# Thirty-two experts on one core: up product ahead of its branch, transposes behind the other branch, down projection and gather between the two

## The chip, the cores and the metric

The kernel runs on one core of a Trainium2 chip, in one launch. The metric is the device time in microseconds, as the median of three runs of the kernel before: 2683.01 us (2674.14 to 2686.55).

## The reference, cut to what matters

Five transformer layers over 256 tokens of width 1024 come first; the change doesn't touch them. The last layer ends in a mixture of 32 experts, in which each token goes to 4:

```python
def clamped_swiglu(hgu):
    gate, up = jnp.split(hgu, 2, axis=-1)
    gate = jnp.minimum(gate, SWIGLU_LIMIT)
    up = jnp.clip(up, -SWIGLU_LIMIT, SWIGLU_LIMIT)
    return gate * jax.nn.sigmoid(SWIGLU_ALPHA * gate) * (up + 1)
...
    logits = (xt @ w_router + b_router).astype(jnp.float32)
    top_v, top_e = lax.top_k(logits, TOP_K)
    gates = jax.nn.softmax(top_v, axis=-1)
...
    def expert_block(args):
        xb, e = args
        return clamped_swiglu(xb @ w1[e] + b1[e]) @ w2[e] + b2[e]
```

Per expert w1 is 1024x2048 and w2 1024x1024, in float32, 12 MB together. How many tokens an expert has is known only at run time, from 0 to 256.

## The kernel before, in words

`experts` (from L1639) unrolls the 32 experts. An expert's tokens stand in slots of 32: the first 32 are always worked on (the main part), the others only inside branches `tc.If(n > 32)`, with inner ones for more than 64, 96 and 128 (`up_others` L1893, `down_others` L1875). Every engine evaluates the branch for itself from its own register. For expert e:

- `gather` (L1683) picks the rows of the tokens of two experts with one-hot matrices `Pq`, as products into a bank `g`; `modulate` (L1505) brings them into `xq`. `prep` (L1837) does half a pair in each step: part 0 in even experts, part 1 in odd ones, the latter followed by `prepare_sum` (L1848: `slot_gates`, `transposed`).
- `bias` (L1574) opens the accumulation in a bank `hg`, `up_proj` (L1728) adds x @ w1: 32 calls, 64 instructions of TensorE, on column quarters.
- `act_more`/`swiglu` (L1736): five instructions, VectorE and ScalarE in turn, from the bank into `um`. The main part fills rows 0 to 63 of `um`, the branch rows 64 to 127.
- `act_T` (L1744) transposes `um`, main and branch rows together, on TensorE, and copies the result into `aT`.
- `down` (L1857): `down_proj` of expert e-1 from `aT` into a bank `py` (64 instructions), its multiply by gate (L1868) and the split into two parts `ye`. `down_others(e-1)` does the other tokens, inside its branch, and adds them to `y` (`sum_more`).
- `scatter` (L1766): for a finished pair of experts, 32 products with the transposed one-hots into four banks, added to `y` by `take_in` (L1764).

The loop (L1932) traces them in this order: up branch of e, main up product, swiglu, down of e-1, down branch of e-1, bias of e+1, transposes, `prep`, on even e `scatter`. The engines' order is not the traced one: a scheduler picks, at build time, the instruction of highest priority (first traced) that is ready by its model; a branch is scheduled as one unit, with all that it reads. In the order that results, 56 of the 64 up instructions run ahead of the up branch and 8 behind it (those of the last weight chunk), and the transposes stand after a quarter of the down projection. `tc.issue_after(x)` puts instructions behind x on x's engine.

`announce` (L1723) issues a branch hint on TensorE's sequencer, behind a given instruction: that the jump over the branch is likely. Labels are `up{e}`, `down{e}` and the inner `down{e}.1`.

Weights come in chunks of 1 MB through a ring of 18 buffers, in SP's queue (`wload` L1399; w1 of e+1 ahead of w2 of e). A buffer is free when all its readers are done, the branch among them. PSUM banks: `hg` x2, `py` x2, `g` x2, and `hg0`, `hg1`, which belong to the branches (`banks` L1872).

Of the kernel before, what the change touches and what calls it, by code (L numbers as in the profile page):

```python
# [9 lines left out]
F32 = mybir.dt.float32  # L10
# [41 lines left out]
def tile_model(ctx: ExitStack, tc: tile.TileContext, A, out):  # L52
# [27 lines left out]
    ident = cb[:, 0:128]  # L80
# [54 lines left out]
    def mm(o, l, r, start=True, stop=True):  # L135
        return T.matmul(o, l, r, start=start, stop=stop)  # L136
# [1320 lines left out]
    def quarter(c):  # L1457
        return slice(32 * c, 32 * c + 32)
# [103 lines left out]
        V.tensor_scalar(rt["gate"][:, t], gr, left, None, ALU.mult)  # L1562

    def new_P():
        return rt["pool"].tile([128, 2, 128], F32, name="P2", tag="P2", bufs=2)

    def slices(j):
        return slice(64 * j, 64 * j + 64)
# [11 lines left out]
    def gtile():  # L1580
        return rt["pe"].tile([128, 512], F32, name="g", tag="g", bufs=2)

    def ytile():
        return rt["pe"].tile([128, 512], F32, name="py", tag="py", bufs=2)
# [54 lines left out]
    def experts(pos, gate, num):  # L1639
        h = xc  # L1640
        with ExitStack() as st:
# [110 lines left out]
            def down_proj(p, aT, e, c0=0, cs=range(4)):  # L1752

                first = None
                for kk in range(8):
                    for c in cs:
                        i = mm(p[quarter(c)], aT[:, kk % 4, c0 + 32 * (kk // 4):c0 + 32 * (kk // 4) + 32], w2_tile(e, kk, c), kk == 0, kk == 7)
                        first = first or i
                return first, i

            def take_in(c, p):

                cols = y[:, :, 256 * c:256 * c + 256]
                return V.tensor_tensor(cols, cols, p.rearrange("p (a b) -> p a b", b=256), op=ALU.add)  # L1764

            def scatter(gTs, yes):  # L1766

                ps = [ytile() for _ in range(2)] + [gtile() for _ in range(2)]
                for t in range(2):
                    for j in range(2):  # L1770
                        for i, part in enumerate(yes):
                            for c in range(4):
                                mm(ps[c][:, 256 * t:256 * t + 256], gTs[quarter(c), j, 128 * t:128 * t + 128], part[quarter(c), j], i + j == 0, i + j == 2)
                for c in range(4):
                    take_in(c, ps[c])


            def new_P1():
# [75 lines left out]

            yes = {}

            def down(e, aT):  # L1857

                j = e % 2
                if j == 0:  # L1860
                    yes[e // 2] = [ep.tile([128, 2, 256], F32R, name=f"ye{nm}", tag=f"ye{nm}") for nm in "hl"]
                gs = gTs[e // 2][1]
                while len(w2s.get(e, ())) < 4:
                    wload()
                p = ytile()[:, 0:256]
                _, last = down_proj(p, aT, e)
                w = ep.tile([128, 512], F32, name="gm", tag="gm")[:, 0:256]
                V.scalar_tensor_tensor(w, p, gs[:, 2 * j:2 * j + 1], g2, ALU.mult, ALU.mult)  # L1868
                two_parts(*[u[:, j] for u in yes[e // 2]], w)
                return last  # L1870

            def banks():  # L1872
                return [pe.tile([128, 512], F32, name=f"hg{g}", tag=f"hg{g}") for g in range(2)]
# [1 line left out]
            def down_others(e, aT, hg=None):  # L1875

                n, ums, ps = conds[e], umss[e % 2], banks()
                with tc.If(n > 32, label=f"down{e}"):
                    p = ps[1][:, 0:256]
                    announce(down_proj(p, aT, e, 64)[0], f"down{e}.1")  # L1880
                    bks = ps if hg is None else [ps[0], hg, ps[1]]
                    j = e % 2
                    sum_more(Pq[e // 2], 64 * j + 32, p, gTs[e // 2][1][:, 2 * j + 1:2 * j + 2], bks)
                    with tc.If(n > 64, label=f"down{e}.1"):
                        announce(down_more(e, 1, 0, ums[:, 0], ps), f"down{e}.2")
                        with tc.If(n > 96, label=f"down{e}.2"):  # L1886
                            announce(down_more(e, 1, 1, ums[:, 0], ps), f"down{e}.3")
                            with tc.If(n > 128, label=f"down{e}.3"):
                                for j in (2, 3):
                                    for g in range(2):  # L1890
                                        down_more(e, j, g, ums[:, j - 1], ps)

            def up_others(e):  # L1893

                n, ums, ps = conds[e], umss[e % 2], banks()
                with tc.If(n > 32, label=f"up{e}"):  # L1896
                    announce(bias(e, ps[0]), f"up{e}.1")
                    up_proj(w1s[e], ps[0], xq[e // 2][:, :, 64 * (e % 2) + 32:64 * (e % 2) + 64])
                    act_more(ps, 0, um, 1)
                    with tc.If(n > 64, label=f"up{e}.1"):  # L1900
                        announce(gather_more(e, 1, ps[1]), f"up{e}.2")
                        up_more(e, ps, 0)
                        act_more(ps, 0, ums[:, 0])
                        with tc.If(n > 96, label=f"up{e}.2"):
                            announce(up_more(e, ps, 1), f"up{e}.3")
                            act_more(ps, 1, ums[:, 0])
                            with tc.If(n > 128, label=f"up{e}.3"):
                                for j in (2, 3):
                                    gather_more(e, j, ps[1])
                                    for g in range(2):  # L1910
                                        up_more(e, ps, g)
                                        act_more(ps, g, ums[:, j - 1])
# [19 lines left out]
            for e in range(32):  # L1932
                hg = nxt
                while len(w1s.get(e, ())) < 8:
                    wload()
                if e == 0:
                    count(0)
                up_others(e)
                i = up_proj(w1s[e], hg, xq[e // 2][:, :, 64 * (e % 2):64 * (e % 2) + 32])
                if e:  # L1940
                    announce(i, f"down{e - 1}")
                if e == 0:
                    prepare_sum(0)
                act_more([hg], 0, um)
                nxt = htile() if e < 31 else None
                if e:
                    down(e - 1, aT)
                    down_others(e - 1, aT, nxt)
                if e < 31:
                    count(e + 1)  # L1950
                    announce(bias(e + 1, nxt), f"up{e + 1}")
                aT = act_T(um)
                if e < 30:
                    prep(e // 2 + 1, e % 2)
                if e:
                    if e % 2 == 0:
                        scatter(gTs.pop(e // 2 - 1)[0], yes.pop(e // 2 - 1))
                    if e == 20:
                        add_b2(umss[1])
                    if e == 30:  # L1960
                        ends = prepare_end(umss[1])
# [259 lines left out]
```

## Time and profile before

| what | value |
|---|---|
| median of 3 runs | 2683.01 us |
| the profiled execution | 2680.88 us |
| its span, first to last instruction | 2679.1 us |
| TensorE products, busy in the span | 2268.7 us (85%) |
| VectorE, ScalarE | 1208.1 us (45%), 714.7 us (27%) |
| the experts, 1285 to 2679.1 us | 1394 us |
| TensorE busy in these | 1052.74 us |
| mean granted clock in these | 0.82 (0.898 in the whole span) |
| mean DMA share and rate in these | 0.70, 281 GB/s |

PE is TensorE's products, PEld its weight loads, DVE VectorE, ACT ScalarE; a trailing q is an engine's sequencer. An idle time in a row is that of the engine ahead of the row's instructions, and behind the arrow stands what ended it: an engine with tile and line, a DMA, a sequencer, or "issue", where the profile shows nothing that was waited for. A product in float32 is two instructions in the trace. The granted clock is 1 at 2.4 GHz and 0.5 at 1.2 GHz.

### The profile page before, as it was taken

The page shows a single profiled execution, that of the slowest core. Times are in us where ns is not written, and L with a number is a line of the kernel's source. Part 1 is how long each engine was busy: PE and PEld are TensorE (multiplying, and loading weights), DVE is VectorE, ACT ScalarE, POOL GpSimd, SP SyncE. Part 2 cuts the span into 40 slices and gives each one's busy share as a digit, 9 for nine tenths or more (in the row PEclk, how much of TensorE's full clock was granted, in tenths as well). Part 3 has the DMA queues.
Part 4 walks back from the last instruction along what each step waited for, and adds up shares of the span by engine and source line. Part 5 has one row for each costly group of instructions (what it writes and reads, how often), then busy time and mean ns, then how long its engine had stood idle before and what let it go on. Part 6 is the DMA issues. An engine that isn't in the chain of part 4 may idle for free. (4 is left out here: it accounts for less than half of the span.)

```text
span 2679.1 us, 43271 instructions
## 1 busy us (share of the span) xinstructions
PE 2268.7 (85%) x17714; PEld 1491.4 (56%) x17714; DVE 1208.1 (45%) x2598; ACT 714.7 (27%) x1578; POOL 80.8 (3%) x125
## 2 busy tenths in 40 slices
PE   7999999989999998899887777877787776777776
PEld 4667777777897876785443343433343443433333
DVE  4877566576656886755322222222223232322222
ACT  4555544443345665424100000000000000000001
POOL 0000200000001000120000000000000000000000
PEclk9999999999999998999978888799887787787878
DMA  7434233333323554714774674599946274599966
GB/s 276 156 122 164 94 114 101 111 133 120 119 64 127 169 195 160 253 70 183 298 302 190 244 304 189 211 380 375 372 197 274 106 295 173 227 406 414 413 281 237
DMA packets 124861, 577.21 MB, mean 215 GB/s; under 512 B 11953, under 2 KB 12721, under 8 KB 91762
## 3 DMA queue, kind: packets, MB, share of 16 engines
q1 hardware_dynamic: 124530, 572.71, 56.3%
q8 instruction: 219, 3.59, 0.5%
q14 instruction: 112, 0.92, 0.1%
HBM read 571.61 MB, written 1.05 MB: 214 GB/s over the span
## 5 line engine op out<-in xcount | busy, mean ns | idle before, releaser
L136 PE MATMUL hg<-w,xq 128*32 128x512 f32 x2944 | 406.6, 664 | 40.6 <-PEq L1896 14.8
L136 PE MATMUL mm<-hT,wp 128*128 128x256 f32 (+1 forms) x1776 | 347.2, 340 | 0.6 <-DVE aqk L144 0.5
L136 PEld LDWEIGHTS mm<-hT,wp 128*128 128x128 f32 x1776 | 269.9, 189 | 52.8 <-issue 19.5
L136 PEld LDWEIGHTS hg<-w,xq 128*32 128x32 f32 x2944 | 112.5, 120 | 281.6 <-issue 236.5
L1738 DVE TENSOR_SCALAR gm<-hg 64x512 f32<-64x512 f32 x51 | 34.8, 683 | 416.3 <-PE hg L136 410.7
L111 DVE TENSOR_TENSOR wp<-w,wp 128x1024 fp32r<-128x1024 f32 (+2 forms) x149 | 177.7, 1198 | 71.7 <-ACT wp L110 70.5
L136 PE MATMUL mm<-wp,hT 128*128 128x256 f32 (+1 forms) x1584 | 194.0, 281 | 6.7 <-DVE mixT L419 3.0
L136 PEld LDWEIGHTS mm<-wp,hT 128*128 128x128 f32 x1584 | 187.0, 189 | 12.5 <-DVE wp L111 3.4
L110 ACT ACTIVATE wp<-w 128x1024 fp32r<-128x1024 f32 (+2 forms) x149 | 153.8, 1036 | 97.8 <-PE mm L136 50.1
L1739 ACT ACTIVATE um<-gm 64x512 f32<-64x512 f32 x46 | 28.9, 629 | 543.2 <-DVE gm L1738 543.2
L136 PE MATMUL py<-w,aT 128*32 128x256 f32 x2048 | 163.0, 445 | 6.5 <-issue 3.5
L136 PEld LDWEIGHTS py<-w,aT 128*32 128x32 f32 x2048 | 73.3, 128 | 85.4 <-issue 54.9
L136 PE MATMUL g<-P,xc 128*128 128x128 f32 x496 | 102.5, 381 | 20.7 <-issue 12.9
L1748 PE MATMUL g<-cb,um 128*128 128x128 f32 x128 | 30.4, 382 | 101.6 <-DVE um L1742 101.6
L136 PEld LDWEIGHTS g<-P,xc 128*128 128x128 f32 x496 | 94.0, 287 | 31.3 <-issue 26.7
L1512 DVE TENSOR_SCALAR xq<-g,modA,modB 128x128 f32<-128x128 f32 x62 | 25.4, 409 | 168.7 <-PE g L136 153.3
L1510 ACT ACTIVATE xq<-g,modB,modA 128x128 f32<-128x128 f32 x62 | 28.3, 457 | 271.3 <-DVE xq L1512 271.3
L136 PE MATMUL hg<-w,aT 128*32 128x256 f32 x896 | 64.5, 429 | 32.1 <-issue 32.1
L136 PE MATMUL ada<-w,scT 128*32 128x512 f32 x576 | 83.4, 623 | 6.6 <-DMA w<-l_w_ada 6.5
L1748 PEld LDWEIGHTS g<-cb,um 128*128 128x128 f32 x128 | 19.6, 190 | 113.3 <-issue 61.9
L136 PE MATMUL hg<-w,xs 128*32 128x512 f32 (+1 forms) x640 | 72.8, 615 | 3.1 <-ACTq L1886 1.1
L136 PE MATMUL hg<-ye,xs 32*128 32x256 f32 x304 | 53.0, 442 | 26.2 <-DVE xl L1764 14.3
(605 smaller groups left out, 3500.4 us busy)
## 6 DMA issues: line engine op xcount, KB each, us to landing
w<-w SPq DMA_DIRECT2D x383, 1024.0 KB, 14.1
w<-l_w_ada SPq DMA_DIRECT2D x96, 512.0 KB, 4.4
w<-w_ada SPq DMA_DIRECT2D x48, 512.0 KB, 4.2
w<-l_w_z SPq DMA_DIRECT2D x32, 512.0 KB, 4.3
w<-l_w_out SPq DMA_DIRECT2D x32, 512.0 KB, 4.1
w<-l_w_q SPq DMA_DIRECT2D x16, 512.0 KB, 5.0
w<-l_w_v SPq DMA_DIRECT2D x12, 512.0 KB, 5.5
w<-w_dqkv SPq DMA_DIRECT2D x12, 512.0 KB, 4.5
```

The costliest lines, as they stand in the source:

```text
L110: S.activation(hi, src, AF.Copy)
L111: V.tensor_tensor(lo, src, hi, op=ALU.subtract)
L136: return T.matmul(o, l, r, start=start, stop=stop)
L1510: S.activation(dst[:, i, :], src[:, i, :], AF.Identity, scale=a[:, k], bias=b[:, k])
L1512: V.tensor_scalar(dst[:, i, :], src[:, i, :], a[:, k], b[:, k], ALU.mult, ALU.add)
L1738: V.tensor_scalar(gm, gate, 7.0, None, ALU.min)
L1739: S.activation(um, gm, AF.Sigmoid, scale=1.702)
L1748: T.transpose(tp[:, q * 128:(q + 1) * 128], um[:, q * 128:(q + 1) * 128], ident)
```

## The change

The main up product and its swiglu are traced ahead of the up branch. The bank `p` of the down projection is claimed ahead of that branch, and the branch writes a column of it, so that the down projection stays behind the branch. Between the two branches stand, in this order: on odd e from 3 to 29 the scatter of the pair before last (it was on even e), now in the branches' two banks and two of `g`; the down projection of e-1; behind its last product the gather of `prep`. After the down branch come bias of e+1, the up hint, and behind the bias the transposes of e. The down hint of e-1 goes behind the first product of scatter or down; the inner hint `down{e}.1` behind the last product of the branch's down projection instead of the first. `P2` has three buffers instead of two. Expert 30 still scatters at its end.

```diff
-        return rt["pool"].tile([128, 2, 128], F32, name="P2", tag="P2", bufs=2)
+        return rt["pool"].tile([128, 2, 128], F32, name="P2", tag="P2", bufs=3)
...
             def scatter(gTs, yes):
-                ps = [ytile() for _ in range(2)] + [gtile() for _ in range(2)]
+                ps, first = banks() + [gtile() for _ in range(2)], None
...
-                                mm(ps[c][:, 256 * t:256 * t + 256], gTs[quarter(c), j, 128 * t:128 * t + 128], part[quarter(c), j], i + j == 0, i + j == 2)
+                                k = mm(ps[c][:, 256 * t:256 * t + 256], gTs[quarter(c), j, 128 * t:128 * t + 128], part[quarter(c), j], i + j == 0, i + j == 2)
+                                first = first or k
...
+                return first
...
-            def down(e, aT):
+            def down(e, aT, p):
...
-                p = ytile()[:, 0:256]
-                _, last = down_proj(p, aT, e)
+                first, last = down_proj(p, aT, e)
...
-                return last
+                return first, last
...
-                    announce(down_proj(p, aT, e, 64)[0], f"down{e}.1")
+                    announce(down_proj(p, aT, e, 64)[1], f"down{e}.1")
...
-            def up_others(e):
+            def up_others(e, p=None):
...
                 with tc.If(n > 32, label=f"up{e}"):
+                    if p is not None:
+                        mm(p[:, 0:1], ident, ident[:, 0:1])
...
-                up_others(e)
-                i = up_proj(w1s[e], hg, xq[e // 2][:, :, 64 * (e % 2):64 * (e % 2) + 32])
+                up_proj(w1s[e], hg, xq[e // 2][:, :, 64 * (e % 2):64 * (e % 2) + 32])
+                act_more([hg], 0, um)
+                p = ytile()[:, 0:256] if e else None
+                up_others(e, p)
+                nxt = htile() if e < 31 else None
+                first = last = None
+                if e % 2 and e > 1:
+                    first = scatter(gTs.pop(e // 2 - 1)[0], yes.pop(e // 2 - 1)) if e < 31 else None
                 if e:
-                    announce(i, f"down{e - 1}")
-                if e == 0:
+                    i, last = down(e - 1, aT, p)
+                    announce(first or i, f"down{e - 1}")
+                    with tc.issue_after(last.ins):
+                        if e < 30:
+                            prep(e // 2 + 1, e % 2)
+                    down_others(e - 1, aT, nxt)
+                else:
                     prepare_sum(0)
-                act_more([hg], 0, um)
-                nxt = htile() if e < 31 else None
-                if e:
-                    down(e - 1, aT)
-                    down_others(e - 1, aT, nxt)
+                    prep(1, 0)
                 if e < 31:
                     count(e + 1)
-                    announce(bias(e + 1, nxt), f"up{e + 1}")
-                aT = act_T(um)
-                if e < 30:
-                    prep(e // 2 + 1, e % 2)
+                    i = bias(e + 1, nxt)
+                    announce(i, f"up{e + 1}")
+                    with tc.issue_after(i.ins):
+                        aT = act_T(um)
+                else:
+                    aT = act_T(um)
                 if e:
-                    if e % 2 == 0:
+                    if e == 30:
                         scatter(gTs.pop(e // 2 - 1)[0], yes.pop(e // 2 - 1))
```

## Rows read from the trace of the kernel before

**Rows 1.** The page: span, and the granted clock in 40 slices, in tenths.

```profile
span 2679.1 us, 43271 instructions
...
PEclk9999999999999998999978888799887787787878
```

**Rows 2.** Waits of TensorE, 1285 us to the end: total us, times, longest.

```profile
PE g L1748 <- DVE um L1742: 101.6, 31, 5.2
...
PE hg L136 <- PEq L1878: 33.2, 14, 4.6
...
PE hg L136 <- PEq L1896: 14.8, 14, 4.2
...
PE hg L136 <- DVE um L1741: 11.6, 4, 2.9
```

**Rows 3.** Timeline of TensorE around a taken branch: start us, us, idle before.

```profile
1403.90 7.04 PE L136 MATMUL hg<-w,xq 128*32 128x512 f32 x62
...
1412.37 1.05 PE L136 MATMUL py<-w,aT 128*32 128x256 f32 x16
1418.58 1.09 PE L1748 MATMUL g<-cb,um 128*128 128x128 f32 x4 [5.15 <-DVE um L1742]
1419.46 2.77 PE L136 MATMUL g<-P,xc 128*128 128x128 f32 x12
1422.16 1.94 PE L136 MATMUL py<-w,aT 128*32 128x256 f32 x16
...
1424.79 1.07 PE L136 MATMUL py<-w,aT 128*32 128x256 f32 x16
```

**Rows 4.** Timeline of TensorE behind a skipped branch.

```profile
1533.91 1.08 PE L1748 MATMUL g<-cb,um 128*128 128x128 f32 x4 [2.85 <-DVE um L1742]
```

**Rows 5.** Timeline of VectorE at the wait of Rows 3.

```profile
1413.10 0.69 DVE L1741 TENSOR_SCALAR um<-hg 64x512 f32<-64x512 f32 x1
...
1414.93 0.68 DVE L1738 TENSOR_SCALAR gm<-hg 64x512 f32<-64x512 f32 x1 [0.41 <-DVEq L1900]
...
1417.75 0.68 DVE L1742 SCALAR_TENSOR_TENSOR um<-um,gm 64x512 f32<-64x512 f32 x1
```

**Rows 6.** Groups of TensorE, 1285 us to the end: busy, mean ns | idle before.

```profile
L136 PE MATMUL hg<-w,aT 128*32 128x256 f32 x896 | 64.5, 429 | 32.1 <-issue 32.1
...
L136 PE MATMUL py<-yeh,gTq 32*128 32x256 f32 x120 | 32.2, 379 | 9.2 <-DVE gm L1868 9.2
...
L136 PE MATMUL hg<-cb,P 128*32 128x128 f32 x304 | 17.6, 289 | 5.5 <-issue 5.5
```

**Rows 7.** Stretches: length, busy PE, PEld, DVE, ACT, POOL, clock, DMA share, GB/s.

```profile
1418.60:1424.20 5.60, 5.60 (x33) 4.11 (x34) 0.00 (x0) 0.00 (x0) 0.00 (x0) 0.50 1.03 416
1533.90:1537.00 3.10, 3.09 (x15) 3.10 (x16) 0.00 (x0) 0.00 (x0) 0.00 (x0) 0.51 0.91 330
1784.00:1945.00 161.00, 120.77 (x1233) 62.73 (x1236) 41.11 (x80) 12.36 (x25) 0.00 (x0) 0.87 0.94 377
2360.00:2560.00 200.00, 145.55 (x1387) 72.24 (x1382) 45.35 (x92) 16.08 (x32) 0.00 (x0) 0.81 1.02 413
2200.00:2350.00 150.00, 112.73 (x1116) 59.73 (x1119) 40.84 (x82) 9.63 (x19) 0.00 (x0) 0.79 0.56 221
```

**Rows 8.** Waits of TensorE, 2360 to 2560 us.

```profile
PE g L1748 <- DVE um L1742: 13.5, 6, 2.9
```

**Rows 9.** Waits of TensorE, 1784 to 1945 us.

```profile
PE g L1748 <- DVE um L1742: 9.6, 3, 4.4
```

**Rows 10.** Branch evaluations on TensorE's sequencer: ns min/median/max, first and last start.

```profile
L1896 PEldq COMPARE_BRANCH  x32: 74/412/6217, 1297.6 to 2639.9; - x32
...
L1878 PEldq COMPARE_BRANCH  x32: 74/400/5626, 1329.7 to 2667.9; - x32
...
L1884 PEldq COMPARE_BRANCH  x24: 69/198/369, 1340.5 to 2623.0; - x24
```

## The prediction

> **What bounds the kernel now.** I read the page first. The span is 2679.1 us, and from the slice at 20 of 40 on (the experts, 1285 us to the end; their first up branch is evaluated at 1297.6 [rows 10]) the granted clock of TensorE is 7 to 8 tenths where it was 9 before [rows 1]. The profiled execution took 2680.88 us, 1.8 us more than its span and 2.1 us less than the median of the runs, 2683.01. Next the waits of TensorE in the experts' stretch: the largest by far is that of the activation transposes of `act_T` for the last swiglu instruction (L1742 on VectorE), 101.6 us in 31 waits [rows 2]. The timeline of TensorE shows how one arises: the up product ends, 16 quarter-instructions of the down projection run in about 1 us, and then the queue stands still until `um` is there: 5.15 us where the second branch ran (an expert with more than 32 tokens), 2.85 us where it was skipped [rows 3, 4]. The reader is to see that the rest of the down projection and the gather, which need no `um`, stand behind the waiting transposes. The timeline of VectorE says why the wait is longer after a branch: the branch's own swiglu comes first, so that the main one starts at 1414.93 and ends at 1418.43, 7 us after TensorE had finished the branch's products [rows 3, 5].
>
> **The up product in front and the transposes at the end.** Nothing is computed less: the edit moves. After it, the main swiglu (about 3.5 us from its first instruction to its last, by the gap between 1414.93 and the end of the 1417.75 row [rows 5]) runs beside the branch or, where that is skipped, beside the down projection and the gather. The down projection is 64 instructions, and 16 take 1.07 us at the full clock, so 4.3 us; the gather of 16 instructions takes at least 3 us (12 of them 2.77 us) [rows 3]. Together 7 us in front of the transposes against 3.5 us of swiglu, and after a taken branch 7 us against the branch's own swiglu of about 3.5 us, the main one having run beside the branch's 62 products of 7.04 us. So I take the whole wait off: **-101.6**. If the scheduler, which orders by readiness, put the branch's swiglu still ahead of the main one, 7 us would stand against 7 us, so this term hardly depends on it.
>
> **The scatter.** It now stands on odd experts ahead of the down projection and writes the two banks `hg0`, `hg1`, which the branch's swiglu still reads. What is late next there: its first product must wait until the clip of `up` (L1741) has read the bank. The trace has that wait in one place, the second products inside the branch: 11.6 us in 4, 2.9 each [rows 2]. Fourteen experts take the branch (896 down products of 64 each in the branches [rows 6]), seven of them are odd and have a scatter (3, 7, 13, 15, 17, 19 and 29 by the timeline's branches): 7 x 2.9 = **+20**. Behind it wait down, gather and the branch on TensorE. In exchange the old scatter's wait for its `py` bank (9.2 us in all [rows 6]) goes: **-9**. VectorE's four additions of 512 columns after the scatter stand ahead of the multiply that empties the down projection's bank; at 0.7 us each, like the swiglu's steps of 512 columns [rows 5], they fit into that projection's 4.3 us: nothing.
>
> **The clock.** After each wait the granted clock is at its half level: 0.50 over the 5.6 us after the long wait, 0.51 over 3.1 us after the short one, with TensorE busy throughout [rows 7]; the same 16 products take 1.94 us there and 1.07 us a little later [rows 3]. So a long wait costs 2.8 us more, a short one 1.5. Thirteen long (over 4 us) and 17 short would be 62 us. I take 25: the seven scatter waits keep 1.5 each, the stretches below that are bound by DMA keep theirs, and instruction stalls nearby can hold the clock down. Bounds 0 and 62: **-25**.
>
> **The weights.** From 2360 to 2560 us the DMA share is 1.02 at 413 GB/s and from 1784 to 1945 it is 0.94 at 377 [rows 7]; a weight ring cannot give more there, so what TensorE saves it waits for the next chunk. These stretches hold 13.5 and 9.6 us of the 101.6 [rows 8, 9]. Earlier stretches leave the ring full, which could cover some; I give all back: **+23** (bounds 0 and 23, plus their part of the clock, counted above). The rest of the ring's order is as before: w1 chunks are still freed at the end of the up branch, w2 chunks at the end of the down branch, so SP's queue is not passed by anything.
>
> **The inner announcement.** Between the branch's down products TensorE stands for 32.1 us, released by nothing that the profile shows, and for 5.5 us more among the transposing products just behind [rows 6]. I take it for waiting for code: instructions come by DMA, in packets of 16 KB (219 of them are 3.59 MB [rows 1]). Today the hint for the inner jump is issued with the first product, and my reading is that the fetch it asks for goes ahead of the code about to run. Issued behind the last product it lets this code through first, which could give all 37.6 us. But the inner jump follows only some 4 us later, and a jump whose target isn't there has cost up to 6.2 us [rows 10]. It is skipped 10 times (24 evaluations, 14 first and 10 second [rows 10]). Half the stalls gone, 10 jumps late by 1.5 us: -19 + 15, **-4**; bounds -38 and +46 (10 x 4.6, the longest wait behind a down jump [rows 2]).
>
> **The other announcements.** The up hint now has the transposes and 64 products (136 instructions with the weight loads) ahead of its branch; the experts' waits behind these jumps are 14.8 us now [rows 2]. Before, the scatter stood in between on half of the experts. I add **+10**; bounds -15 and +55 (18 skipped branches x 4.2 us less the present wait). The down hint on odd experts is as far ahead of its branch as now, with the scatter added, so I leave the 33.2 us behind that branch [rows 2] as they are. What the hints are worth can be read: all evaluations of the inner branch, ten jumps among them, took 0.37 us at most, while the up and the down branch, hinted as well, took up to 6.2 and 5.6 us [rows 10]. So a hint helps in some places and is lost in others.
>
> The Trainium skill (Runtime: NRT & Kernel Launch, section Instruction fetch mechanics) says that instructions are prefetched in sequence only, two pages at a time, and that a jump out of these pages waits for a fetch. By that rule alone the hints would be worth nothing before and after, both announcement terms would be zero, the sum -92.6 and the time 2590 us; the trace's ten cheap inner jumps [rows 10] disagree, so the terms stay and rival (c) below has its chance from them.
>
> **Small ones together.** A third `P2` buffer, one 1-column product in each taken branch (14 in all, each shorter than the 0.29 us of a 128-column one [rows 6]), the claimed `py` bank (freed long before): nothing; even in full the products are 4 us.
>
> **Sum:** -101.6 + 20 - 9 - 25 + 23 - 4 + 10 = -86.6 us, so 2680.9 - 87 = 2594 on the profiled execution, and 2 us more on the median: **2596 us**.
>
> **Rivals.** (a) More comes back: half of the scatter waits is filled, the clock gives 45 instead of 25, the inner stalls go without late jumps (-30 instead of -4), the full ring covers half of the weights' part: 87 + 10 + 20 + 26 + 12 = 155, 2528 us. For it: the clock's level follows the waits in every row read. Against it: it takes four kind outcomes at once. (b) The weights take more: with experts coming faster, stretches that are now at half of the DMA, as 2200 to 2350 us at 0.56 [rows 7], become full as well where light experts lie in them. Of the 101.6 us then only the heavy experts' 13 long waits count, about 62 us, less 20 and with 10 of clock: 52, 2631 us. (c) The other side, **late jumps**: the place is the sequencer of TensorE at L1884, L1896 and L1878. If hints so close to their branch do nothing, each of 10 inner, 18 up and 9 even down skips (37) can cost 4.6 us and 1.5 us of half clock. The other terms give 101.6 - 20 + 9 + 25 - 23 = 93 us, so it decides from 15 late places on; at 20 places the time is 2683 + 122 - 93 = 2712 us. For it: up branches already take up to 6.2 us although they are hinted [rows 10]. Against it: the up hint of even experts and the down hint of even experts keep about as many instructions ahead of their branch as now. (d) The order isn't what the source says: the scheduler moves down and transposes so that TensorE waits for `um` again. The branch's product into `p` and the after-orders speak against it; then about 2683 us, no change.
>
> **Chances.** Forecast 0.58, (a) 0.14, (b) 0.14, (c) 0.08, (d) 0.06. Half a per cent (13 us) is what a measurement of this kernel can tell from no change. The first three are faster: 0.86; (d) is the same, 0.06; (c) slower, 0.08. The range leaves out (c), (d) and the outer part of (a): 2525 to 2660, from the sum with the kind ends of clock and inner hint to (b) with the up hint's dear half.
>
> **What would show it.** In the new profile the row L1748 <- L1742 should fall from 101.6 to a few us; the scatter's first products should show waits for L1741 of 2.9 in seven places; the granted clock of the work that now fills 2200 to 2350 us (0.79 now [rows 7]) should rise; "DMA w<-w" should grow as a releaser of up products; the 32.1 us between the branch's down products should halve, with waits named PEq L1884 in their place. The prediction is wrong if the L1748 wait stays above 40 us, or if PEq waits grow by more than 60 us, or if the wait moves to the `aT` copy or to the gather's one-hots.

## The result, and the profile after

The kernel after takes 2540.92 us (2537.56 to 2550.62), the kernel before, run beside it, 2678.57 us (2671.01 to 2686.55): a ratio of 0.949, with a 95% interval of 0.945 to 0.953. That is 5.1% faster. It lies inside the predicted range, 55 us below the predicted 2596 us, and nearer to rival (a). The profiled execution took 2538.24 us, 142.6 less than the one of before.

In the profile after some lines have moved: the up branch is L1897 (its swiglu parts L1903, L1907, L1910), the down branch L1879 (inner L1885, L1887, L1889), and the down projection's multiply L1869. The page, to set beside [rows 1]:

```profile
span 2536.5 us, 43274 instructions
...
PEclk9999999998999999999898788888888888788787
```

The clock of the experts' stage, from slice 20 on, has risen by less than a tenth. The stage is best weighed by stretches. The whole experts' stage of the kernel before (length, busy PE, PEld, DVE, ACT, POOL, clock, DMA share, GB/s):

```profile
1287.00:2679.00 1392.00, 1050.74 (x10209) 537.17 (x10208) 352.60 (x681) 108.87 (x214) 1.99 (x4) 0.82 0.70 281
```

and with only the instructions counted that touch the scatter's `gTq` (no POOL among them):

```profile
1287.00:2679.10 1392.10, 88.02 (x512) 65.65 (x512) 6.21 (x9) 4.56 (x8) 0.82 0.70 281
```

The same two views of the kernel after, the stage:

```profile
1297.00:2536.50 1239.50, 994.48 (x10235) 494.68 (x10234) 350.09 (x679) 106.50 (x213) 1.99 (x4) 0.84 0.79 315
```

and the scatter's part:

```profile
1297.00:2537.00 1240.00, 64.74 (x512) 54.08 (x512) 6.22 (x9) 4.56 (x8) 0.84 0.79 315
```

TensorE stood for 1392.0 - 1050.7 = 341.3 us before and for 1239.5 - 994.5 = 245.0 after: 96 us less. It was busy for 56 us less with the same products (but for the 1-column ones in the branches), 23 of them in the scatter. The stage began 10 us later in this execution, which the change doesn't touch. -96 - 56 + 10 is, but for rounding, the 142.6.

Waits of TensorE in the stage, after, to set beside [rows 2]:

```profile
PE g L136 <- issue: 38.4, 13, 5.2
PE hg L136 <- issue: 22.2, 10, 6.1
PE g L136 <- PEq L1879: 19.3, 9, 3.9
PE py L136 <- DMA w<-w: 19.1, 15, 2.8
PE hg L136 <- DVEq L1903: 16.2, 6, 2.7
PE hg L136 <- DVEq L1897: 14.0, 6, 3.2
...
PE hg L136 <- DMA w<-w: 12.9, 13, 1.5
PE hg L136 <- DVE um L1741: 11.7, 4, 2.9
PE py L136 <- PEq L1897: 10.8, 14, 2.7
PE g L136 <- PEq L1885: 9.1, 9, 5.4
```

The largest row of before, 101.6 us of transposes waiting for the swiglu, is gone from the list. Groups of TensorE in the stage, after (busy, mean ns | idle before), to set beside [rows 6]:

```profile
L136 PE MATMUL hg<-w,xq 128*32 128x512 f32 x2944 | 383.4, 630 | 13.0 <-DMA w<-w 12.9
...
L136 PE MATMUL hg<-w,aT 128*32 128x256 f32 x896 | 57.5, 404 | 13.5 <-issue 13.5
...
L136 PE MATMUL hg<-yeh,gTq 32*128 32x256 f32 x124 | 27.4, 387 | 34.1 <-DVEq L1903 16.2 <-DVEq L1897 14.0 <-DVEq L1910 2.7
...
L1748 PE MATMUL g<-cb,um 128*128 128x128 f32 x128 | 26.4, 339 | 5.5 <-DVEq L1903 3.8 <-issue 1.8
L136 PE MATMUL g<-gate,P 128*32 128x1 f32 x1024 | 16.5, 186 | 28.7 <-issue 28.7
```

The transposes (L1748) still stand for 5.5 us. The scatter's first products (`hg<-yeh,gTq`) have a new wait of 34.1. The gate products of the gather waited before for ScalarE and hardly for anything unseen:

```profile
L136 PE MATMUL g<-gate,P 128*32 128x1 f32 x1024 | 11.7, 174 | 13.5 <-ACT xq L1510 13.0 <-issue 0.4
```

They now stand 28.7 us for nothing that the profile shows.

How the cover works is seen on VectorE, at the expert of [rows 3] and [rows 5], after:

```profile
1394.04 0.68 DVE L1738 TENSOR_SCALAR gm<-hg 64x512 f32<-64x512 f32 x1 [5.00 <-PE hg L136]
...
1396.87 0.68 DVE L1742 SCALAR_TENSOR_TENSOR um<-um,gm 64x512 f32<-64x512 f32 x1
1401.56 0.68 DVE L1738 TENSOR_SCALAR gm<-hg 64x512 f32<-64x512 f32 x1 [4.01 <-PE hg L136]
```

and on TensorE at the same time, with the place where the branch ends:

```profile
1394.44 7.04 PE L136 MATMUL hg<-w,xq 128*32 128x512 f32 x64
...
1405.28 0.75 PE L136 MATMUL hg<-yeh,gTq 32*128 32x256 f32 x2 [2.69 <-DVEq L1903]
```

The main swiglu ends at 1397.55, while the branch's products run until 1401.5. What TensorE waits for behind the branch is now the branch's own swiglu, which frees the bank for the scatter: 2.69 us in place of 5.15.

### The profile page after: what moved, and what is told of

It is laid out like the page before. It is cut to its first block, busy times and chain, and to the rows that moved or that the text cites. A ratio compares the mean times of both kernels' runs of the same rounds, so it can differ in the third digit from the quotient of the medians.

```text
span 2536.5 us, 43274 instructions
## 1 busy us (share of the span) xinstructions
PE 2225.5 (88%) x17740; PEld 1456.0 (57%) x17740; DVE 1206.3 (48%) x2598; ACT 712.8 (28%) x1577; POOL 80.1 (3%) x125
## 5 line engine op out<-in xcount | busy, mean ns | idle before, releaser
L136 PE MATMUL hg<-w,xq 128*32 128x512 f32 x2944 | 383.4, 630 | 13.0 <-DMA w<-w 12.9
L136 PEld LDWEIGHTS hg<-w,xq 128*32 128x32 f32 x2944 | 94.4, 114 | 231.0 <-issue 192.4
L136 PEld LDWEIGHTS py<-w,aT 128*32 128x32 f32 x2048 | 87.1, 127 | 128.9 <-issue 76.9
L1764 DVE TENSOR_TENSOR xl<-xl,hg 128x512 f32<-128x512 f32 x108 | 69.6, 684 | 74.8 <-PE hg L136 72.5
L136 PE MATMUL g<-P,xc 128*128 128x128 f32 x496 | 76.9, 301 | 31.2 <-PEq L1879 19.3
L136 PEld LDWEIGHTS g<-P,xc 128*128 128x128 f32 x496 | 64.3, 202 | 54.3 <-issue 54.1
L110 ACT ACTIVATE yeh<-gm 128x256 fp32r<-128x256 f32 x31 | 12.9, 417 | 234.9 <-DVE gm L1869 234.9
L136 PE MATMUL hg<-ye,xs 32*128 32x256 f32 x304 | 52.0, 434 | 26.9 <-DVE xl L1764 13.5
L136 PE MATMUL hg<-w,aT 128*32 128x256 f32 x896 | 57.5, 404 | 13.5 <-issue 13.5
L136 PE MATMUL s<-wp,oz 128*128 128x512 f32 x264 | 64.2, 392 | 0.0
```

The costliest lines, as they stand in the source:

```text
L110: S.activation(hi, src, AF.Copy)
```

## The experiments

### Which of the moves carries the gain

The kernel before with one order added: the transposes go behind the last product of the down projection.

```diff
-                    down(e - 1, aT)
+                    last = down(e - 1, aT)
...
-                aT = act_T(um)
+                if e:
+                    with tc.issue_after(last.ins):
+                        aT = act_T(um)
+                else:
+                    aT = act_T(um)
```

> The kernel before with one order alone changed: the transposes of the activations behind the last product of the down projection instead of behind its first quarter; up product, scatter, gather and hints stay. 48 more down instructions (3.2 us at the full clock) stand ahead of them. Theory (the wait and the clock that falls behind it are the gain): the 17 short waits go and the 13 long ones keep about 1.9 us, so some 25 of 101.6 us stay; with about 35 us of clock, 2675 - 77 - 35 = 2563 us. Rival 1 (the clock does not follow the wait): 2675 - 77 = 2598 us. Rival 2 (the order of the other parts carries the gain): above 2620 us.

Measured: 2536.82 us (2526.68 to 2554.11) against 2672.62, ratio 0.947 (0.940 to 0.954), which is the kernel after's own. What is left of the wait:

```profile
PE g L1748 <- DVE um L1742: 27.6, 18, 2.6
```

So this order alone gives as much as the whole change, with 27.6 us of the wait left, where only the down projection covers the swiglu and not the gather. The time is 26 us below the theory's 2563. The stage as a stretch shows where:

```profile
1300.00:2552.20 1252.20, 1010.47 (x10204) 538.51 (x10203) 350.99 (x678) 108.96 (x214) 1.99 (x4) 0.83 0.78 312
```

TensorE stands for 241.7 us in place of 341.3, 100 less: 74 of the wait itself, as expected, and 17 of the gather's waits for ScalarE and VectorE, which the expectation left out. It is busy for 40 us less with the same products, 3 of them in the scatter (88.0 to 84.7). The mean clock gives some 75 us less at the half level (0.82 over 1392 us, 0.83 over 1252; each mean is rounded to a hundredth, which is worth 14 us), half of which is 38. So where one order alone is changed, the clock comes back with the wait, by about the 35 us expected.

The kernel before with the other half alone, the main up product and its swiglu traced ahead of the up branch:

```diff
-                up_others(e)
                 i = up_proj(w1s[e], hg, xq[e // 2][:, :, 64 * (e % 2):64 * (e % 2) + 32])
+                act_more([hg], 0, um)
+                up_others(e)
...
-                act_more([hg], 0, um)
```

> The kernel before with the main up product and its swiglu ahead of the up branch, nothing else; the transposes still stand ahead of most of the down projection. Theory (where the transposes stand decides): the wait hardly falls, as a taken branch leaves its own swiglu of 3.5 us and a skipped one some 2.3 us: 13 x 3.5 + 17 x 2.3 = 85 of 101.6 us, so 2675 - 17 - 8 of clock = 2650 us. Rival (the up product's place is what matters): the wait halves, 2675 - 50 - 25 = 2600 us.

Measured: 2621.25 us (2620.33 to 2632.26), ratio 0.981 (0.974 to 0.988). The transposes still wait, under other names:

```profile
PE g L1748 <- DVEq L1896: 37.4, 14, 3.1
PE g L1748 <- DVEq L1900: 37.0, 10, 3.8
...
PE g L1748 <- PEq L1896: 10.0, 3, 4.0
```

101.6 us have become 84.4 in these three rows. What ends the wait now is VectorE's sequencer: at a taken branch behind the branch's own swiglu (L1900), at a skipped one where it passes the branch, which comes behind the main swiglu (L1896). The work that could cover it is still queued behind the transposes. The gain of 51 us, between the theory's 25 and the rival's 75, is larger than these 17 us of waiting. In its profile TensorE stands for 35 us less in the stage and is busy for 33 us less, but its "issue" waits are 73.4 us, no shorter than before; what the rest comes from isn't shown.

The kernel after with that half undone, the up branch traced ahead again:

```diff
-                up_proj(w1s[e], hg, xq[e // 2][:, :, 64 * (e % 2):64 * (e % 2) + 32])
-                act_more([hg], 0, um)
                 p = ytile()[:, 0:256] if e else None
                 up_others(e, p)
+                up_proj(w1s[e], hg, xq[e // 2][:, :, 64 * (e % 2):64 * (e % 2) + 32])
+                act_more([hg], 0, um)
```

> The changed kernel with the up branch traced ahead of the main up product again; transposes, scatter, down, gather and hints stay as changed. Theory (the late transposes carry the gain; the up product's place only decides whether a taken branch's swiglu comes first): no wait of the transposes over 1 us, 2541 within 15 us. Rival (the main swiglu has to run beside the branch): 13 waits of 2 to 3 us come back, with their clock, 2541 + 50 = 2591 us.

Measured: 2522.05 us (2517.01 to 2529.42), ratio 0.943 (0.937 to 0.950): 4 us below the theory's range, and far from the rival's 2591. The longest wait of the transposes for VectorE is 1.5 us; one of 4.3 us is for nothing that the profile shows. The change doesn't need the up product in front of its branch. What counts is that the transposes stand behind other work.

### The inner announcement

Before with the hint behind the last product, and after with it behind the first:

```diff
-                    announce(down_proj(p, aT, e, 64)[0], f"down{e}.1")
+                    announce(down_proj(p, aT, e, 64)[1], f"down{e}.1")
```

> The kernel before with the inner hint alone moved behind the last down product. Theory: 32.1 + 5.5 us of idle time in and behind the branch's down products fall to half and the clock gains a little: about 2679 - 25 = 2654 us. Rival: the fetch is only late in another place (the inner jump, the code behind it): 2679 within 8 us.

> The changed kernel with one part undone: the inner hint again behind the first down product of the branch. Theory (the late hint lets the code of the branch through first): the idle time between the branch's down products goes from 13.5 back to some 30 us, with some clock, so about 2541 + 25 = 2566 us. Rival (the late hint gives nothing, the shorter idle time there comes from other code positions): 2541 within 8 us, and the idle time stays near 13 us or moves elsewhere.

Measured: before with the late hint 2670.74 us, ratio 0.998 (0.995 to 1.001); after with the early one 2546.02 us, ratio 0.953 (0.949 to 0.956). Neither can be told from its twin. In the kernel after the stalls between the branch's down products are 13.5 us with the late hint and 14.6 with the early one (`hg<-w,aT`, waits "issue"), so their fall from 32.1 [rows 6] isn't the hint's doing. Nor are the late inner jumps that appear. Evaluations of the inner branch in the kernel after:

```profile
L1885 PEldq COMPARE_BRANCH  x24: 69/197/6067, 1350.4 to 2478.0; - x24
```

and with the early hint:

```profile
L1885 PEldq COMPARE_BRANCH  x24: 69/197/3312, 1339.1 to 2471.4; - x24
```

The longest was 0.37 us before [rows 10]; now single ones take 6.1 and 3.3 us, with either place of the hint.

### The scatter

The kernel after with the scatter on even experts again, in its old banks:

```diff
-                ps, first = banks() + [gtile() for _ in range(2)], None
+                ps, first = [ytile() for _ in range(2)] + [gtile() for _ in range(2)], None
...
-                if e % 2 and e > 1:
-                    first = scatter(gTs.pop(e // 2 - 1)[0], yes.pop(e // 2 - 1)) if e < 31 else None
...
-                    if e == 30:
+                    if e % 2 == 0:
```

> The changed kernel with the scatter where it was before: on even experts, at their end, in the two py and the two g banks. Theory: the 34 us of waiting for the branches' banks go, 9 us of waiting for a py bank come back, so about 2541 - 25 - 8 of clock = 2508 us. Rival (the scatter between the branches is what covers the swiglu on odd experts): the transposes' wait for um comes back on odd experts with a taken branch by 1 to 3 us each, 2530 to 2550 us.

Measured: 2534.92 us (2528.62 to 2538.33), ratio 0.948 (0.944 to 0.953): the move is worth nothing that shows, and the theory's 2508 is missed. The wait for the branches' banks is gone, but other waits are longer: behind jumps 69.2 us in all for 49.6 in the kernel after, for weights 38.8 for 32.0, "issue" 78.5 for 68.4. The rival's number came, its mechanism didn't: the transposes' wait is 3.8 us.

The kernel after with the scatter behind the last product of the down projection, still on odd experts:

```diff
-                if e % 2 and e > 1:
-                    first = scatter(gTs.pop(e // 2 - 1)[0], yes.pop(e // 2 - 1)) if e < 31 else None
                 if e:
                     i, last = down(e - 1, aT, p)
+                    if e % 2 and 1 < e < 31:
+                        with tc.issue_after(last.ins):
+                            scatter(gTs.pop(e // 2 - 1)[0], yes.pop(e // 2 - 1))
```

> The changed kernel with the scatter of odd experts behind the last down product instead of ahead of the first. Theory (the scatter's 34 us of waiting for the branches' banks is idle time on the path, and the granted clock falls behind it): the wait goes to nearly nothing and the time by 34 us and some 10 of clock, 2541 - 44 = 2497 us. Rival (the weights already set the pace): waits for w take most of it, 2525 to 2541 us.

Measured: 2506.38 us (2502.85 to 2517.0), ratio 0.939 (0.935 to 0.943), below both kernels. The bank wait is gone, and the gather, now the next to want the `g` banks, has one of the same size:

```profile
PE g L136 <- DVE xl L1764: 33.5, 14, 2.4
```

So the wait only changed its place. What did fall is the scatter itself. Its products alone, in the stage (columns as above, without POOL):

```profile
1289.00:2502.00 1213.00, 26.39 (x512) 20.69 (x512) 6.22 (x9) 4.56 (x8) 0.84 0.80 322
```

26.4 us where the kernel after has 64.7, for the same 512 instructions. The timeline of TensorE at one scatter shows how:

```profile
1398.01 0.39 PE L136 MATMUL hg<-yeh,gTq 32*128 32x256 f32 x2
1398.02 0.38 PE L136 MATMUL g<-yeh,gTq 32*128 32x256 f32 x2
1398.23 0.28 PE L136 MATMUL hg<-yel,gTq 32*128 32x256 f32 x1
1398.24 0.28 PE L136 MATMUL g<-yel,gTq 32*128 32x256 f32 x1
...
1401.62 0.78 PE L136 MATMUL g<-P,xc 128*128 128x128 f32 x3 [2.39 <-DVE xl L1764]
```

Four products on four quarters of 32 rows run side by side, all 32 within 1.2 us. In the kernel after the scheduler had issued the two bank pairs at different times, and only one quarter pair is in flight together (the row at 1405.28 above is one of eight such steps of 0.2 us, for half a scatter). The clock has a part in it too. The two halves of that scatter in the kernel after, and the whole one in this kernel (columns as above):

```profile
1385.90:1387.80 1.90, 1.84 (x16) 1.66 (x16) 0.00 (x0) 0.00 (x0) 1.00 1.02 410
1405.20:1407.50 2.30, 2.22 (x16) 1.98 (x16) 0.00 (x0) 0.00 (x0) 0.50 1.00 413
1398.00:1399.24 1.24, 1.22 (x32) 1.02 (x32) 0.00 (x0) 0.00 (x0) 1.00 0.99 410
```

At the full clock 16 products take 1.84 us there and all 32 take 1.22 here; the half behind the wait for the bank runs at the half clock. Counting all scatter products of the stage by the clock granted while they ran (an estimate from the clock records of the traces), they would take 66.9 us at the full clock in the kernel before, 45.2 in the kernel after and 24.7 here. So of the 38 us between 64.7 and 26.4, some 20 are the order of issue and some 18 the clock, and of the 23 us between 88.0 and 64.7, 22 are the order.

The Trainium skill (TensorE: Matmul & The Clock Gate, section Part 3: Packing small matmuls) says that products on different tiles of the array run concurrently, and that a weight load overlaps products in flight only where its row group differs. For the first, this timeline agrees: 32 products of some 0.28 us each end within 1.2 us. The second no run here tests. In these two timelines the four quarters overlap only where their products are issued next to each other.

The same with the fourth bank from `py` instead of `g`, so that one `g` bank stays free for the gather:

```diff
-                ps, first = banks() + [gtile() for _ in range(2)], None
+                ps, first = banks() + [gtile(), ytile()], None
```

> The kernel with the scatter behind the down projection, and its fourth bank the free py bank instead of the second g bank, so that the gather behind it finds a bank. Theory (the gather's 33.5 us of waiting for the additions to y are idle time on the path): 2506 - 33 - 8 of clock = 2465 us. Rival (the weights set the pace from here on): waits for w grow by 15 us or more, 2480 to 2506 us.

Measured: 2509.27 us (2500.87 to 2524.98), ratio 0.939 (0.931 to 0.946), so the expectation of a gain was missed. The gather's bank wait fell from 33.5 to 5.3 us, but waits behind the down branch's jump came in its place:

```profile
PE hg L136 <- PEq L1879: 40.4, 9, 6.6
...
PE g L136 <- PEq L1879: 21.4, 8, 4.9
```

61.8 us, where the same jump had 28.5 with the other bank. Both together are no shorter than before.

The last one puts the up branch ahead again (the edit of late_only) and the scatter behind the down projection (that of scatter_behind_down).

> The kernel after with the up branch traced ahead of the main up product again (as in late_only) and the scatter behind the last product of the down projection (as in scatter_behind_down). Theory, the two gains have different places (less waiting behind the up branch's jump there, a shorter scatter here) and add up: 2506 less up to 19, 2487 to 2500. Rival, late_only was no faster than the kernel after in truth, as their intervals touch: 2506 within 8.

Measured: 2524.5 us (2506.86 to 2534.97), ratio 0.943 (0.939 to 0.947). The short scatter is there again (26.6 us), but the sum of the two gains isn't: this kernel is no faster than late_only, and its interval overlaps that of scatter_behind_down. The theory falls, and the rival's number is missed as well.

### The clock: work in place of the wait

The kernel before, its order on TensorE written out in the code, and a twin with 16 more transposes of the identity ahead of those that wait:

```diff
-                for q in range(4):
-                    T.transpose(tp[:, q * 128:(q + 1) * 128], um[:, q * 128:(q + 1) * 128], ident)
+                for q in range(FILL):
+                    T.transpose(tp[:, q % 4 * 128:q % 4 * 128 + 128], ident, ident)
+                for q in range(4):
+                    i = T.transpose(tp[:, q * 128:(q + 1) * 128], um[:, q * 128:(q + 1) * 128], ident)
...
-                _, last = down_proj(p, aT, e)
+                _, quarter_end = down_proj(p, aT, e, kks=range(2))
+                with tc.issue_after(quarter_end.ins):
+                    tp, i = transposes(um)
+                with tc.issue_after(i.ins):
+                    _, last = down_proj(p, aT, e, kks=range(2, 8))
```

> The kernel before with its order on TensorE written out: behind the first quarter of the down projection stand the transposes of act_T, and behind the transposes the rest of the down projection. That is the order that the scheduler had chosen before by itself, so both theories expect the kernel before within 10 us, and a wait of the transposes for the last swiglu instruction of 100 us within 15. It is the twin of the next run.

> The twin, with 16 more transposes of the identity per expert into the bank of the transposes, ahead of those that wait (512 more instructions on TensorE, whose result is overwritten): TensorE works in the wait instead of standing. Nothing leaves the path but the wait itself, whose length the swiglu still sets. Theory, the granted clock follows these waits and is a gain of its own: the half-clock time falls by some 40 to 90 us as it did where the transposes were moved, and half of that comes back, so 20 to 45 us less than the twin, though the added products run beyond the wait in some experts and cost up to 10. Rival, the clock is set by something else and the gain of the change was the wait alone: the same as the twin or up to 20 us more (16 products of 0.16 to 0.27 us, where the wait is shorter than that).

Measured: the twin without filling (FILL = 0) 2636.21 us (2628.36 to 2662.05), ratio 0.983 (0.979 to 0.988); with it (FILL = 16) 2643.62 us (2639.36 to 2650.58), ratio 0.988 (0.983 to 0.992). Without filling, the wait among TensorE's waits:

```profile
PE g L1750 <- DVE um L1743: 90.7, 27, 5.2
```

and the stage as a stretch:

```profile
1298.00:2660.30 1362.30, 1038.81 (x10207) 522.00 (x10204) 352.13 (x681) 108.87 (x214) 1.99 (x4) 0.83 0.72 287
```

With filling, the wait:

```profile
PE g L1750 <- DVE um L1743: 46.0, 22, 3.2
```

the added products among the groups:

```profile
L1748 PE MATMUL g<-cb 128*128 128x128 f32 x512 | 67.6, 288 | 0.9 <-issue 0.9
```

and the stage:

```profile
1292.00:2643.20 1351.20, 1077.39 (x10719) 566.70 (x10719) 351.37 (x681) 107.98 (x214) 1.98 (x4) 0.85 0.72 289
```

67.6 us of useless products were added and 38.6 us of busy time came with them, so the other products became 29 us shorter. The mean clock rose from 0.83 over 1362 us to 0.85 over 1351: about 58 us less at the half level (twice the missing share times the length), half of which is the same 29. So the clock of the work behind goes with these waits. The size is rough: each mean is rounded to a hundredth, worth 14 us, and the profiled execution of the unfilled twin has the lowest clock of its five (0.896 over the whole span; the other four have 0.900 to 0.910, the filled one's four 0.908 to 0.912). What it is worth in time this pair doesn't settle: only 44.7 us of the wait were filled, the rest of the products ran beyond it, the intervals overlap, and the theory's 20 to 45 us less didn't come. And the unfilled twin, with the order of before unchanged but for expert 1, was 41 us faster than before and so missed its expectation.

### What the place of the code is worth

The kernel before with 48 transposes of the identity once, at expert 0, so that all later code lies 96 instructions further on:

```diff
+                for q in range(shift):
+                    T.transpose(tp[:, q % 4 * 128:q % 4 * 128 + 128], ident, ident)
...
-                aT = act_T(um)
+                aT = act_T(um, 48 if e == 0 else 0)
```

> The kernel before with 48 more transposes of the identity, once, ahead of the transposes of expert 0, into their bank: with their weight loads 96 instructions more on TensorE, some 6 us of work, after which all code of the experts lies 96 instructions further on. The order is the same from expert 2 on. The question is how much of the time hangs on where the code lies, since the twin of the filled wait came out 41 us below the kernel before with its order unchanged but for expert 1. Theory, the waits for code and the half-clock stretches behind them fall elsewhere, and that moves the time by 15 to 45 us either way, beyond the added 6. Rival, the place of the code is worth nothing: 2683 within 8, and the 41 us of the twin come from the split itself.

Measured: 2633.95 us (2621.6 to 2651.78) against 2671.8, ratio 0.986 (0.981 to 0.990): 38 us faster with more work and, from expert 2 on, the same order. That is the size that the theory gave. TensorE's waits for nothing that the profile shows, in the stage, before:

```profile
PE hg L136 <- issue: 48.2, 14, 6.6
...
PE g L136 <- issue: 13.3, 4, 5.0
...
PE py L136 <- issue: 8.3, 3, 4.8
```

and with the code moved:

```profile
PE hg L136 <- issue: 30.5, 10, 6.4
...
PE g L136 <- issue: 2.6, 1, 2.6
```

The three of before are 69.8 us, these two (and one of 0.7) 33.8: 36 us less. The two profiled executions are 29 us apart, the medians 38. The transposes' wait is as long as ever (103.9 us), and so are the waits for weights (11.9 us for 12.3), so the added work didn't gain its time by letting the weights run ahead. How far two executions differ with the code nearly in place is seen in before_inner_last: 64.3 us. So in this displacement the stalls went with where the instructions lie, and I take them for waiting for code, which comes by DMA in packets of 16 KB; that last step is argued, not shown. Nor does it explain the twin: its "issue" waits are 63.1 us, 7 less than before, so what made it 41 us faster stays open. The page of the kernel before, on its instruction queue (packets, MB, share), which is the source of the prediction's 219 packets:

```profile
q8 instruction: 219, 3.59, 0.5%
```

## Why the prediction was right, and where it was off

**The wait** is the step that decided, and it held: -101.6 predicted, 101.6 to 5.5 measured. Its mechanism, that the rest of the down projection stood behind the waiting transposes, is shown by the run that moves the transposes and nothing else: 74 of the 101.6 us go there. That the gather covers the rest is argued from the 27.6 us left in that run and the 5.5 here. The up product's move, which the prediction counted as part of it, is not needed.

**The scatter's bank wait** was the right mechanism at too few places: 34.1 us against 20. The prediction counted the seven odd experts with a taken branch at 2.9. The trace has 13 places, since where the branch is skipped VectorE's sequencer passes its branch only behind the main swiglu ("DVEq L1897", 14.0 in 6). The old wait of 9.2 went as predicted. Unseen was that the scatter's products would take 64.7 us instead of 88.0: -23. They do so with the scatter back on even experts too (65.1), so it isn't the banks or the odd experts. By the estimate at the full clock, 66.9 and 45.2, it is nearly all the order in which the quarters are issued.

**The weights** came out as sized: waits for `w` 12.3 us before (9.9 and 2.4), 32.0 after, +20 against +23.

**The clock** was sized at 25 with bounds of 0 and 62. The busy time outside the scatter fell by 56 - 23 = 33 us; by the mean clock (0.82 over 1392 us, 0.84 over 1239.5) some 104 us less were spent at the half level, half of which would be 52 if TensorE had been busy in all of it. So 33 to 52; the mechanism held, as the run with the transposes alone shows (37 us less busy outside the scatter), and the term was too small. That the half level follows each wait, as the prediction has it, is nearly but not quite so: behind waits of 2.3, 2.3 and 1.2 us (at 1845.9, 2357.8 and 2647.6 us in the kernel before) the granted clock was 1.00 over the next 3 us. The stretch from the transposes of expert 19 to those of expert 22, 159 us at 0.80 before, takes 105 us at 0.85, with a DMA share of 0.73 for 0.58: as the prediction wanted to see it, and not the full DMA of rival (b). Before, and after:

```profile
2199.00:2358.00 159.00, 119.08 (x1172) 62.51 (x1173) 43.59 (x86) 10.26 (x20) 0.00 (x0) 0.80 0.58 231
...
2135.00:2240.00 105.00, 89.42 (x879) 45.86 (x879) 35.35 (x72) 8.91 (x18) 0.00 (x0) 0.85 0.73 293
```

**The announcements** are the term with the wrong sign. I had +10 for the up branch and nothing for the down branch. Waits behind the up jump went from 20.9 us (14.8 [rows 2], and 6.1 ahead of the gather) to 10.8, behind the down jump from 33.2 to 21.0: -22. How much of that belongs to the change isn't settled: in inner_first, which differs from the kernel after by the place of the inner hint alone and takes the same time, the same two jumps hold 16.0 and 29.8, only 8 less than before. Rival (c) didn't come. The inner hint's -4 was a guess at something that isn't there: two runs show no effect, the stalls between the down products fell and turned up ahead of the gate products, "issue" as a whole stayed (69.8 before, 68.4 after), and waits behind the inner jump rose from 4.4 to 9.6. The rule of the Trainium skill that the prediction weighed (Runtime: NRT & Kernel Launch, section Instruction fetch mechanics), that a jump out of the prefetched pages waits for a fetch, fits the hinted inner jumps of up to 6.1 us that the kernel after has and the one before had not.

**Not costed at all** were the gather's waits for ScalarE and VectorE (13.0 for `xq`, 3.9 for `gsq`), which are gone: -17. They are gone too where the transposes alone are moved, and remain where the up product alone is.

In sum TensorE's idle time fell by 96 us where the terms said 62 (-101.6 + 20 - 9 + 23 - 4 + 10), its busy time by 56 where they said 25, and the stage began 10 us later. That the result is near rival (a) is not that rival's doing: of its four outcomes only the clock came. The rest is the shorter scatter, the jumps and the gather. These three, 62 us together, were not foreseen and all fell on the same side, with the longer scatter wait (+14) and the inner jumps (+5) against them; that the time stayed inside the range, 16 us above its lower end, is in part luck.

**What limits all of this** is the last experiment. The prediction took 13 us for what a measurement can tell from no change. That holds for the medians of one kernel (2671.8 to 2683.0 for the kernel before); an edit also moves code, and one such move alone was worth 38 us here. The gain of the change stands far above it, and it isn't luck of that kind, since the "issue" stalls are as long after as before. But the terms that are jumps are not separated from it, nor are the differences among the variants: the 51 us of the up product alone, the 19 of late_only, the 34 of the scatter behind the down projection. Against the unfilled twin, a kernel with the order of before, the one order that carries the gain is worth 2636 - 2537 = 99 us; against the kernel before, 136. Which of the two is the fairer figure stays open, and whether scatter_behind_down is faster than the kernel after for its scatter or for its code as well.

## What to carry to other kernels

Look for work without a need for the late result that stands in the same queue behind an instruction that has one; the name of the wait tells what is late, the rows behind it what could run. Before a gain of 1 to 2% is put down to an edit, move the code by some instructions without an edit, and compare the "issue" waits of both profiles. Products on different row quarters should be issued next to each other; if the scheduler pulls them apart, tie them to one point at which all their banks are free.

## What was not expected of the hardware

Moving code by 96 instructions changed the stalls without a visible cause from 69.8 to 33.8 us and the time by 38 us. The same 512 products of 32 rows took 88.0, 64.7 or 26.4 us by how they were issued and at which clock; at the full clock it would be some 67, 45 and 25. An inner jump hinted in the same way took 0.37 us at most in one kernel and up to 6.1 in another.
